# ScalarE copies the last quarter before the new weights in two gate-and-up units of each feed-forward block, and the last down unit adds its kept quarters in a step of its own

## The chip, the core and the metric

The kernel runs on one core of a Trainium2 chip. A core has five engines that run side by side and wait for each other through semaphores: TensorE (PE, matrix products into PSUM; PEld is its weight loads), VectorE (DVE), ScalarE (ACT), GpSimd (POOL) and SyncE (SP, which here only issues DMAs). Each engine takes its instructions in the order in which the program holds them. The metric is the device time of one execution in microseconds. Three runs of the kernel before took 1720.83, 1725.48 and 1731.36 us; their median is 1725.48 us.

## The reference, cut to what matters

Two layers, each with a feed-forward block (FFN), a mixer (convolution and differential attention) and a second FFN; so there are four FFNs. `x` is 512 x 1024, the hidden width `D_FF` is 2816.

```python
def swiglu(h, w_gate, w_up, w_down):
    return (jax.nn.silu(h @ w_gate) * (h @ w_up)) @ w_down
...
    for l in range(DEPTH):
        x = x + 0.5 * swiglu(rms_norm(x, ffn1_norm[l]), ffn1_w_gate[l], ffn1_w_up[l], ffn1_w_down[l])
        h = rms_norm(x, mix_norm[l])
        ...
        x = x + jnp.concatenate([conv_out, diff_out], axis=-1) @ w_out[l]
        x = x + 0.5 * swiglu(rms_norm(x, ffn2_norm[l]), ffn2_w_gate[l], ffn2_w_up[l], ffn2_w_down[l])
    return x
```

## The kernel before

**Precision.** Every float32 operand is split in two rounded parts: ScalarE copies it (`hi`, L375 for the weights of a unit), VectorE takes the rest (`lo`, L379), and TensorE makes three matmuls, hi*hi, hi*lo and lo*hi (`product`, L384 to L394; the matmuls are L392).

**Units.** The 22 tiles of the hidden width are handled in three parts (`PARTS`): 5 plain ones, then 8, then 9. The second and third part are made of *units*. A gate-and-up unit (`GateUp`) makes one hidden tile from 128 columns of the gate and 128 of the up weights; a down unit (`Down`) makes two tiles of the output. A unit is a product of 2 x 2 blocks done with seven block products in place of eight, from sums and differences of the blocks; each product is 4 steps of 3 matmuls on 256 columns. The seven accumulate in the four halves a, d, b, c of two PSUM banks, in this order (`body`, L411 to L446): c, d, then the seventh product of the unit before (`rest`), then a, b, c again ("all") and a again ("g1u2u1"). A half that must be added in twice is copied to SBUF on the way, into four *quarters* of a tile called `keep`: quarter 3 from c (L410), quarters 0 and 1 from a and d (L421), quarter 2 from a after its second product (L442). `rest` of the unit, one unit later, writes into a again, so it must wait until L442 has read a.

**The weights of a unit.** While unit n runs, SyncE loads the weights of unit n+1 (`load`; up L475, gate L476), GpSimd makes four sums of blocks from them (L365 to L368: d, then in place of one up half, then two into the tile `more`), and ScalarE and VectorE split the four operands: A (the up pair, of which the second sum is one half), B (the gate pair), C (`more`, the third and fourth sum) and D (the first sum). The tiles lie in rings: `wraw` has 5 slots and a unit takes three of them (up, gate, more); `whi` and `wlo` have 4 each for A, B and C; D has its own. A slot is given out again in turn, so the up tile of unit n waits for B of unit n-2 to be split, the gate tile of unit n for C of unit n-2, and `more` of unit n for A of unit n-1. The first sum of unit n waits for D of unit n-1 to be split and for the gate tile of unit n.

**What sets the order.** The program is written unit by unit, but a scheduler with a timing model of its own orders the instructions of each engine at build time, except where two are held in the written order (`pinned(..., True)` or `keep_in_program_order`). What it gave for ScalarE and VectorE at the places of the change is shown below. The first matmuls of the products are all held, so the order on TensorE hardly depends on it.

**The places.** A pair of hidden tiles is also summed (`hold`, `combine`), so even and odd units differ a little. The change touches the unit with number n = 3 of the 8 and the one with n = 5 of the 9, in each of four FFNs: eight places. It also touches the last down unit of each FFN, whose `tail` is reversed (a before c): there VectorE in `close` adds quarters 0 and 2 of `keep` to the bank with b and c (L654), adds half of that to one tile of the output `x` (`into`, L644), and `rest` adds to a second tile (L644 again). In the last FFN each tile of `x` is then sent to memory (L1253).

Of the kernel before, what the change touches and what calls it, by code (L numbers as in the profile page):

```python
# [14 lines left out]
AF = mybir.ActivationFunctionType  # L15
ALU = mybir.AluOpType
# [55 lines left out]
def trunk(ctx: ExitStack, tc: tile.TileContext, xt, par, lamv, relb, onehot,  # L72
          gu1, dn1, wag, wqkv, wout, gu2, dn2, out):
    nc = tc.nc
    V, S, G, T = nc.vector, nc.scalar, nc.gpsimd, nc.tensor
# [268 lines left out]
    def pinned(ins, pin=PIN):  # L344
        if pin:
            tc.keep_in_program_order(ins)
        return ins
# [4 lines left out]
    def by_two(t):  # L352
        return t.rearrange("p (n c) -> p n c", n=2)

    class Unit:
# [49 lines left out]
        def body(self, nxt, prev, prev2):  # L405
            if nxt:
                nxt.load()
            self.begin()
            self.go(self.c, "u2u1", "t1", first=True)
            pinned(S.activation(self.keep[:, 3], self.c, AF.Copy))  # L410
            if nxt:  # L411
                nxt.hi("A", isinstance(prev, Down))
                nxt.lo("A")
            self.go(self.d, "u2", "t4", first=True)
            self.early()
            if nxt:
                nxt.hi("B")
            if prev:
                prev.rest()
            self.go(self.a, "g1", "b11")  # L420
            pinned(S.activation(self.keep[:, :2], by_two(self.banks[0]), AF.Copy))  # L421
            if prev:
                prev.finish(0)
            if nxt:
                nxt.lo("B")
            if prev:
                prev.finish(1)
            if nxt:
                nxt.hi("D")
                nxt.lo("D")  # L430
            if prev:
                prev.finish(2)
            self.go(self.b, "g2", "b21")
            self.middle()
            if nxt:
                nxt.hi("C")
            if prev2 and not prev2.soon:
                prev2.combine()
            for ps, *product in self.tail():
                self.go(ps, *product)  # L440
                if ps is self.a:
                    pinned(S.activation(self.keep[:, 2], self.a, AF.Copy), isinstance(self, Down))  # L442
            self.close()
            if nxt:
                nxt.lo("C")
# [18 lines left out]
    class GateUp(Unit):  # L464
# [27 lines left out]
        def close(self):  # L492
            g, two = self.keep[:, 0::2], by_two(self.banks[1])
            pinned(V.tensor_tensor(two, two, g, op=ALU.add))
            pinned(S.activation(g, two, AF.Silu))
# [45 lines left out]
    class Down(Unit):  # L541
# [106 lines left out]
        def close(self):  # L648
            A, B = 2 * self.q, 2 * self.q + 1
            two, keep = by_two(self.banks[1]), self.keep  # L650
            late = self.left and not self.q
            if late:
                self.plain(self.banks[1], 0)
            pinned(V.tensor_tensor(two, two, keep[:, 0::2], op=ALU.add))  # L654
            self.into(A, two, 0.5)
            self.after(A)
            if late:
                self.spare()
            if self.left:
                pinned(V.tensor_tensor(by_two(self.ps), by_two(self.ps), keep[:, 1::2], op=ALU.subtract))  # L660
                self.into(B, by_two(self.ps), 0.5)
# [580 lines left out]
    for l in range(DEPTH):  # L1242
        nxt = {}
# [89 lines left out]
```

## Time and profile before

| what | value |
|---|---|
| the profiled execution, whole | 1723.03 us |
| its span (first to last instruction) | 1721.2 us |
| median of three runs (lowest, highest) | 1725.48 us (1720.83, 1731.36) |
| granted TensorE clock | 1.000 |
| split of unit weights on VectorE, L379, 1024 columns: mean of one | 1454 ns |
| the same on ScalarE, L375, 1024 columns: mean of one | 1062 ns |
| GpSimd's four sums, L365, L366, L367, L368: mean of one | 1221, 1558, 1453, 1523 ns |
| L442, the copy of quarter 2 | 84 times, 352 to 389 ns |

The profiled execution is 2.45 us below the median of the runs. "Idle before" in a row of the profile is the time for which an engine had nothing running just before that instruction, with what ended it. A matmul's row gives its latency; matmuls follow each other faster than they end, so the time of one is read from the distance between starts, or from how many fit in a stretch.

### The profile page before, as it was taken

The page shows a single profiled execution, that of the slowest core. Times are in us where ns is not written, and L with a number is a line of the kernel's source. Part 1 is how long each engine was busy: PE and PEld are TensorE (multiplying, and loading weights), DVE is VectorE, ACT ScalarE, POOL GpSimd, SP SyncE. Part 2 cuts the span into 40 slices and gives each one's busy share as a digit, 9 for nine tenths or more (in the row PEclk, how much of TensorE's full clock was granted, in tenths as well). Part 3 has the DMA queues.
Part 4 walks back from the last instruction along what each step waited for, and adds up shares of the span by engine and source line. Part 5 has one row for each costly group of instructions (what it writes and reads, how often), then busy time and mean ns, then how long its engine had stood idle before and what let it go on. Part 6 is the DMA issues. An engine that isn't in the chain of part 4 may idle for free.

```text
span 1721.2 us, 30788 instructions
## 1 busy us (share of the span) xinstructions
PE 1711.0 (99%) x12013; PEld 1580.8 (92%) x12013; DVE 1404.3 (82%) x2049; ACT 1001.0 (58%) x1607; POOL 894.9 (52%) x664
## 2 busy tenths in 40 slices
PE   9999999999999999999999999999999999999998
PEld 7899999988789899999988999999887888999998
DVE  6988878969766978878968788888688578788887
ACT  6457556645854446656634575665558454565663
POOL 3165555468763146555412566555687531565653
PEclk9999999999999999999999999999999999999999
DMA  7233333433122223333332333334230222333332
GB/s 232 90 113 111 107 109 96 148 106 98 38 74 98 74 98 111 99 120 102 119 103 79 110 107 116 106 111 160 74 111 29 82 87 85 99 116 106 115 107 87
DMA packets 82930, 177.90 MB, mean 103 GB/s; under 512 B 8951, under 2 KB 30726, under 8 KB 82784
## 3 DMA queue, kind: packets, MB, share of 16 engines
q1 hardware_dynamic: 81184, 174.10, 30.6%
q8 instruction: 94, 1.54, 0.4%
q0 software_dynamic: 1312, 1.67, 0.3%
q14 instruction: 52, 0.43, 0.1%
q10 hardware_dynamic: 288, 0.16, 0.0%
HBM read 173.79 MB, written 3.42 MB: 103 GB/s over the span
## 4 chain that ended last, share of the span: by engine, by line
PE 93%; DVE 4%; ACT 1%; issue 1%; DMA 1%; POOL 0%; DVEq 0%; SPq 0%; ACTq 0%
PE ps_pair L392 51%; PE ps_pair L144 6%; PE ps_pair L148 6%; PE ps_pair L147 6%; PE ps_d L144 2%; PE ps_d L147 2%; PE ps_d L148 2%; PE ps_sc L1104 2%; PE ps_out L144 2%; PE ps_out L147 2%; PE ps_out L148 2%; PE ps_pair L980 2%; PE ps_pair L981 2%; PE ps_pair L979 2%; DVE wlo L379 2%; PE ps_o L1134 1%
## 5 line engine op out<-in xcount | busy, mean ns | idle before, releaser
L379 DVE TENSOR_TENSOR wlo<-wraw,whi 128x1024 fp32r<-128x1024 f32 (+1 forms) x400 | 505.0, 1273 | 114.8 <-ACT whi L375 109.0
L375 ACT ACTIVATE whi<-wraw 128x1024 fp32r<-128x1024 f32 (+1 forms) x400 | 375.3, 953 | 215.1 <-PE ps_pair L392 83.2
L365 POOL TENSOR_TENSOR wraw<-wraw 128x512 f32<-128x512 f32 x100 | 122.1, 1221 | 566.1 <-DVE wlo L379 290.0
L392 PE MATMUL ps_pair<-acts,whi 128*128 128x256 f32 x2240 | 393.5, 278 | 0.0
L392 PEld LDWEIGHTS ps_pair<-acts,whi 128*128 128x128 f32 x2240 | 339.8, 188 | 0.4
L392 PE MATMUL ps_pair<-acts,wlo 128*128 128x256 f32 x1120 | 310.8, 278 | 0.0
L392 PE MATMUL ps_pair<-th,whi 128*128 128x256 f32 x816 | 227.1, 278 | 0.4 <-ACT keep L442 0.4
L392 PE MATMUL ps_pair<-tl,whi 128*128 128x256 f32 x816 | 226.5, 278 | 0.0
L392 PE MATMUL ps_pair<-th,wlo 128*128 128x256 f32 x816 | 226.5, 278 | 0.0
L107 ACT ACTIVATE whi<-wraw 128x1024 fp32r<-128x1024 f32 (+3 forms) x124 | 123.5, 1002 | 149.7 <-PE ps_pair L147 83.6
L392 PEld LDWEIGHTS ps_pair<-acts,wlo 128*128 128x128 f32 x1120 | 210.5, 188 | 0.0
L147 PE MATMUL ps_pair<-acts,whi 128*128 128x512 f32 x448 | 174.5, 390 | 0.0
L148 PE MATMUL ps_pair<-acts,wlo 128*128 128x512 f32 x448 | 174.2, 391 | 0.0
L144 PE MATMUL ps_pair<-acts,whi 128*128 128x512 f32 x448 | 173.5, 393 | 0.3 <-ACT whi L107 0.3
L366 POOL TENSOR_TENSOR wraw<-wraw 128x512 f32<-128x512 f32 x100 | 155.8, 1558 | 7.6
L368 POOL TENSOR_TENSOR wraw<-wraw 128x512 f32<-128x512 f32 x100 | 152.3, 1523 | 7.8
L392 PEld LDWEIGHTS ps_pair<-th,whi 128*128 128x128 f32 x816 | 153.2, 188 | 1.2 <-ACT keep L442 0.8
L392 PEld LDWEIGHTS ps_pair<-tl,whi 128*128 128x128 f32 x816 | 154.0, 189 | 0.0
L392 PEld LDWEIGHTS ps_pair<-th,wlo 128*128 128x128 f32 x816 | 153.4, 188 | 0.0
L367 POOL TENSOR_TENSOR wraw<-wraw 128x512 f32<-128x512 f32 x100 | 145.3, 1453 | 7.8
L392 PE MATMUL ps_pair<-hs,whi 128*128 128x256 f32 x704 | 125.3, 278 | 0.0
L1072 DVE SCALAR_TENSOR_TENSOR ps_y<-u,par,ps_y 128x512 f32<-128x512 f32 x156 | 117.6, 754 | 3.8
(220 smaller groups left out, 4080.8 us busy)
## 6 DMA issues: line engine op xcount, KB each, us to landing
wraw<-in_gu SPq DMA_DIRECT2D x172, 512.0 KB, 3.9
wraw<-in_wqkv SPq DMA_DIRECT2D x24, 512.0 KB, 3.8
wraw<-in_wag SPq DMA_DIRECT2D x16, 512.0 KB, 3.8
wraw<-in_wout SPq DMA_DIRECT2D x16, 512.0 KB, 3.6
wraw<-in_dn SPq DMA_DIRECT2D x60, 128.0 KB, 2.9
wraw<-in_dn SPq DMA_DIRECT2D x20, 384.0 KB, 3.2
wraw<-in_dn SPq DMA_DIRECT2D x28, 256.0 KB, 2.9
wraw<-in_dn SPq DMA_DIRECT2D x20, 320.0 KB, 3.0
```

Source lines behind the costliest of these rows:

```text
L107: S.activation(hi, raw, AF.Copy)
L144: first = T.matmul(ps, wh, xh, start=start, stop=False)
L147: T.matmul(ps, wh, xl, start=False, stop=False)
L148: T.matmul(ps, wl, xh, start=False, stop=stop)
L365: G.tensor_tensor(d, g1, u1, op=ALU.add)
L366: G.tensor_tensor(u1, u2, u1, op=ALU.add)
L367: G.tensor_tensor(m0, g1, u1, op=ALU.add)
L368: G.tensor_tensor(m1, g2, m0, op=ALU.add)
L375: pinned(S.activation(hi, raw, AF.Copy), pin)
L379: pinned(V.tensor_tensor(out=lo, in0=raw, in1=f32(hi), op=ALU.subtract), pin)
L392: mm = T.matmul(ps, l, r, start=first and i == n == 0, stop=False, skip_group_check=True)
L1072: V.scalar_tensor_tensor(ys[c] if t == PAD and not n else y, us[c][:, t : t + SEQ], pars[l][:, wc + t : wc + t + 1], y, op0=ALU.mult, op1= ...
```

## The change

Two edits. First, in the unit with n = 3 of the second part and n = 5 of the third, where a gate-and-up unit follows, the copy of C of the next unit is no longer written before the last two products but after them, and L442 and this copy are held in the written order: first quarter 2, then C. Second, in the last down unit of each FFN the addition of quarters 0 and 2 into the PSUM bank is replaced by adding half of them to `x` directly from `keep`, and the bank is added to `x` as before.

```diff
             self.go(self.b, "g2", "b21")
             self.middle()
-            if nxt:
+            swap = isinstance(self, GateUp) and isinstance(nxt, GateUp) and self.n == (3, 5)[self.gated.ahead]
+            if nxt and not swap:
                 nxt.hi("C")
             if prev2 and not prev2.soon:
                 prev2.combine()
             for ps, *product in self.tail():
                 self.go(ps, *product)
                 if ps is self.a:
-                    pinned(S.activation(self.keep[:, 2], self.a, AF.Copy), isinstance(self, Down))
+                    pinned(S.activation(self.keep[:, 2], self.a, AF.Copy), swap or isinstance(self, Down))
+            if swap:
+                nxt.hi("C", True)
             self.close()
             if nxt:
                 nxt.lo("C")
...
-            pinned(V.tensor_tensor(two, two, keep[:, 0::2], op=ALU.add))
+            if self.last:
+                self.into(A, keep[:, 0::2], 0.5)
+            else:
+                pinned(V.tensor_tensor(two, two, keep[:, 0::2], op=ALU.add))
             self.into(A, two, 0.5)
```

**ScalarE at the first place (first FFN, unit n = 3 of the second part).** The unit's keep is `keep_1226`, its banks `ps_pair_1224` (a, d) and `ps_pair_1225` (b, c); `ps_pair_1101` is the unit before (n = 2). `wraw_1219` is C of the next unit (n = 4), `wraw_1348` and `wraw_1349` are A and B of the one after (n = 5). Before:

```order
L421 ACTIVATE keep_1226<-ps_pair_1224 128x512
L375 ACTIVATE whi_1309<-wraw_1219 128x1024
L739 ACTIVATE hold_1287<-ps_pair_1101 128x512
L375 ACTIVATE whi_1374<-wraw_1348 128x1024
L442 ACTIVATE keep_1226<-ps_pair_1224 128x256
L753 ACTIVATE low_183<-ps_pair_1101 128x512
L410 ACTIVATE keep_1360<-ps_pair_1359 128x256
L375 ACTIVATE whi_1390<-wraw_1349 128x1024
L495 ACTIVATE keep_1226<-ps_pair_1225 128x2x256
```

After (lines below the change have moved: L442 is L443, L739 is L745, L753 is L759, L495 is L498):

```order
L421 ACTIVATE keep_1226<-ps_pair_1224 128x512
L745 ACTIVATE hold_1287<-ps_pair_1101 128x512
L759 ACTIVATE low_183<-ps_pair_1101 128x512
L443 ACTIVATE keep_1226<-ps_pair_1224 128x256
L375 ACTIVATE whi_1342<-wraw_1219 128x1024
L375 ACTIVATE whi_1374<-wraw_1348 128x1024
L410 ACTIVATE keep_1360<-ps_pair_1359 128x256
L498 ACTIVATE keep_1226<-ps_pair_1225 128x2x256
L375 ACTIVATE whi_1390<-wraw_1349 128x1024
```

The copies of C (n = 4) and of A (n = 5) have both moved behind the copy of quarter 2; the copy of the hidden tile's parts (L753) has moved ahead of it. The same is so at all eight places.

**VectorE at the same place.** The rows of the unit before, of this one and of the weights. Before:

```order
L502 SCALAR_TENSOR_TENSOR ps_pair_1101<-ps_pair_1101,keep_1103 128x512
L379 TENSOR_TENSOR wlo_1310<-wraw_1219,whi_1309 128x1024
L744 TENSOR_TENSOR ps_pair_1101<-hold_1287,ps_pair_1101 128x256
L379 TENSOR_TENSOR wlo_1375<-wraw_1348,whi_1374 128x1024
L494 TENSOR_TENSOR ps_pair_1225<-ps_pair_1225,keep_1226 128x512
L758 TENSOR_TENSOR low_183<-ps_pair_1101,low_183 128x512
L379 TENSOR_TENSOR wlo_1391<-wraw_1349,whi_1390 128x1024
L500 TENSOR_TENSOR ps_pair_1224<-ps_pair_1224,keep_1226 128x256
L379 TENSOR_TENSOR wlo2_1425<-wraw2_1352,whi2_1424 128x512
L501 TENSOR_TENSOR ps_pair_1224<-ps_pair_1224,keep_1226 128x256
```

After (L744 is L750, L758 is L764, L494 is L497, L500 to L502 are L503 to L505):

```order
L505 SCALAR_TENSOR_TENSOR ps_pair_1101<-ps_pair_1101,keep_1103 128x512
L750 TENSOR_TENSOR ps_pair_1101<-hold_1287,ps_pair_1101 128x256
L764 TENSOR_TENSOR low_183<-ps_pair_1101,low_183 128x512
L497 TENSOR_TENSOR ps_pair_1225<-ps_pair_1225,keep_1226 128x512
L379 TENSOR_TENSOR wlo_1343<-wraw_1219,whi_1342 128x1024
L379 TENSOR_TENSOR wlo_1375<-wraw_1348,whi_1374 128x1024
L503 TENSOR_TENSOR ps_pair_1224<-ps_pair_1224,keep_1226 128x256
L379 TENSOR_TENSOR wlo_1391<-wraw_1349,whi_1390 128x1024
L504 TENSOR_TENSOR ps_pair_1224<-ps_pair_1224,keep_1226 128x256
L379 TENSOR_TENSOR wlo2_1425<-wraw2_1352,whi2_1424 128x512
```

The lo part of C (`wraw_1219`) stood directly behind the last step of the unit before; now it stands three places later, behind the sum that closes unit 3 (L497), which itself waits for quarter 2.

**VectorE at the end of the program (the last down unit, n = q = 3).** `ps_pair_19473` is the bank with b and c, `ps_pair_19472` the one with a. Before:

```order
L660 TENSOR_TENSOR ps_d_19500<-ps_d_19500,keep_19474 128x512
L644 SCALAR_TENSOR_TENSOR x_78<-ps_d_19500,x_78 128x512
L654 TENSOR_TENSOR ps_pair_19473<-ps_pair_19473,keep_19474 128x512
L644 SCALAR_TENSOR_TENSOR x_78<-ps_pair_19473,x_78 128x512
L644 SCALAR_TENSOR_TENSOR x_78<-ps_pair_19472,x_78 128x512
```

After (L660 is L666, L644 is L647):

```order
L666 TENSOR_TENSOR ps_d_19500<-ps_d_19500,keep_19474 128x512
L647 SCALAR_TENSOR_TENSOR x_78<-ps_d_19500,x_78 128x512
L647 SCALAR_TENSOR_TENSOR x_78<-keep_19474,x_78 128x512
L647 SCALAR_TENSOR_TENSOR x_78<-ps_pair_19473,x_78 128x512
L647 SCALAR_TENSOR_TENSOR x_78<-ps_pair_19472,x_78 128x512
```

One instruction is replaced by another in the same place; it no longer reads the bank with b and c. On GpSimd and SyncE nothing moves. On TensorE three matmuls of one step change places with a fourth, once in the program.

## The prediction

> **What bounds the kernel now.** I read the page first, then the waits of TensorE, then its matmul rate by stretches, then the timeline of four engines around one of the eight places. The page's first part:
>
> ```profile
> span 1721.2 us, 30788 instructions
> ...
> PE 1711.0 (99%) x12013; PEld 1580.8 (92%) x12013; DVE 1404.3 (82%) x2049; ACT 1001.0 (58%) x1607; POOL 894.9 (52%) x664
> ```
>
> TensorE is the bound, from end to end; an edit on ScalarE and VectorE can only win what TensorE waits for. Of the seven rows of its waits, this is the one that the change touches:
>
> ```profile
> PE ps_pair L392 <- ACT keep L442: 0.4, 2, 0.2
> ```
>
> Two times, 0.4 us. That undercounts, since a matmul's modelled end covers short gaps. Starts of neighbouring matmuls show more. First at n = 3 in the first FFN of layer 1 and of layer 0, then at n = 5 of both FFNs of layer 1:
>
> ```profile
> 990.09 0.28 PE L392 MATMUL ps_pair<-th,wlo 128*128 128x256 f32 x1
> 990.29 0.38 PE L392 MATMUL ps_pair<-th,whi 128*128 128x256 f32 x1
> ...
> 990.63 0.28 PE L392 MATMUL ps_pair<-th,wlo 128*128 128x256 f32 x1
> ```
>
> ```profile
> 130.55 0.39 PE L392 MATMUL ps_pair<-th,whi 128*128 128x256 f32 x1
> ```
>
> ```profile
> 1123.74 0.28 PE L392 MATMUL ps_pair<-th,wlo 128*128 128x256 f32 x1
> 1124.18 0.38 PE L392 MATMUL ps_pair<-th,whi 128*128 128x256 f32 x1 [0.16 <-ACT keep L442]
> 1124.40 0.28 PE L392 MATMUL ps_pair<-tl,whi 128*128 128x256 f32 x1
> ```
>
> ```profile
> 1645.43 0.39 PE L392 MATMUL ps_pair<-th,whi 128*128 128x256 f32 x1 [0.23 <-ACT keep L442]
> ```
>
> The late matmul is the first of `rest`. What is its cost? That needs the undisturbed rate, from matmuls per stretch:
>
> ```profile
> 95.00:130.00 35.00, 35.00 (x311) 1.00 0.35 112
> 131.00:305.00 174.00, 174.00 (x1480) 1.00 0.32 104
> ...
> 711.00:831.00 120.00, 120.00 (x1022) 1.00 0.33 108
> ...
> 991.00:1123.00 132.00, 132.00 (x1166) 1.00 0.33 109
> ...
> 1512.00:1644.00 132.00, 132.00 (x1165) 1.00 0.33 109
> ```
>
> 132 / 1166 is 113.2 ns a matmul. At 990 three steps took 0.54 us where 0.34 would do: 0.20 lost. At 1123 two took 0.66 for 0.23: 0.43 lost, and by the larger idle time 0.50 at 1645. The other three n = 3 places look like the one at 990, so I take 4 x 0.20 + 0.43 + 0.50 = 1.7 us lost to L442 in the execution.
>
> The same table holds a second thing: 174 / 1480 is 117.6 ns and 120 / 1022 is 117.4, at the same granted clock (1.00, fourth figure). So there is a slow stretch in each FFN of layer 0, together 1480 x 4.4 ns + 1022 x 4.2 ns = 6.5 + 4.3 = 10.8 us, six times the waits. The first begins between 130 and 131, at the late matmul of 130.55; the second begins near 710, where TensorE's waits name nothing. After the n = 3 waits of layer 1, at 990 and just before 1512, the rate stayed at 113.2. So a wait may start a slow stretch (one of the three shown), and a stretch can start without one.
>
> **The first edit.** Why is L442 late? ScalarE and GpSimd around the place at 990:
>
> ```profile
> 984.91 1.06 ACT L375 ACTIVATE whi<-wraw 128x1024 fp32r<-128x1024 f32 x1 [0.59 <-PE ps_pair L392]
> 986.78 0.60 ACT L739 ACTIVATE hold<-ps_pair 128x512 f32<-128x512 f32 x1 [0.81 <-DVE ps_pair L502]
> 988.90 1.06 ACT L375 ACTIVATE whi<-wraw 128x1024 fp32r<-128x1024 f32 x1 [1.52 <-POOL wraw L366]
> 989.87 0.37 ACT L442 ACTIVATE keep<-ps_pair 128x256 f32<-128x256 f32 x1
> ...
> 997.95 1.06 ACT L375 ACTIVATE whi<-wraw 128x1024 fp32r<-128x1024 f32 x1 [1.76 <-POOL wraw L366]
> 998.92 0.36 ACT L442 ACTIVATE keep<-ps_pair 128x256 f32<-128x256 f32 x1
> ```
>
> ```profile
> 985.75 1.09 POOL L365 TENSOR_TENSOR wraw<-wraw 128x512 f32<-128x512 f32 x1 [5.09 <-DVE wlo L379]
> 986.92 1.95 POOL L366 TENSOR_TENSOR wraw<-wraw 128x512 f32<-128x512 f32 x1
> ...
> 994.56 1.10 POOL L365 TENSOR_TENSOR wraw<-wraw 128x512 f32<-128x512 f32 x1 [2.39 <-DVE wlo L379]
> 995.74 2.18 POOL L366 TENSOR_TENSOR wraw<-wraw 128x512 f32<-128x512 f32 x1
> ```
>
> L442 stands behind the copy of A (988.90), which waits for GpSimd's second sum. In the new order only the hold (986.78 to 987.38), a step of VectorE (0.42) and the copy L753 (0.59) stand ahead of L442, so it runs at about 988.4 and ends near 988.75, 1.5 us before TensorE needs it (990.09 + 0.11 = 990.20). The 1.7 us go.
>
> What is late next? The lo part of C. VectorE:
>
> ```profile
> 986.65 1.27 DVE L379 TENSOR_TENSOR wlo<-wraw,whi 128x1024 fp32r<-128x1024 f32 x1
> 987.84 0.42 DVE L744 TENSOR_TENSOR ps_pair<-hold,ps_pair 128x256 f32<-128x256 f32 x1
> 990.00 1.22 DVE L379 TENSOR_TENSOR wlo<-wraw,whi 128x1024 fp32r<-128x1024 f32 x1 [1.74 <-ACT whi L375]
> 991.14 0.69 DVE L494 TENSOR_TENSOR ps_pair<-ps_pair,keep 128x512 f32<-128x512 f32 x1
> ...
> 993.80 0.68 DVE L379 TENSOR_TENSOR wlo<-wraw,whi 128x512 fp32r<-128x512 f32 x1
> ...
> 994.86 0.70 DVE L502 SCALAR_TENSOR_TENSOR ps_pair<-ps_pair,keep 128x512 f32<-128x512 f32 x1
> 995.73 1.23 DVE L379 TENSOR_TENSOR wlo<-wraw,whi 128x1024 fp32r<-128x1024 f32 x1 [0.17 <-ACT whi L375]
> ```
>
> It ended at 987.92 and would now start after the closing sum, at about 989.7. Here a sum of GpSimd and a lo part exclude each other: the sum at 986.92 met the lo part of 986.65 and took 1.95 us for 1.09, ending 0.95 after it; the one at 995.74 took 2.18, ending 0.96 after it. Without a lo part beside them, GpSimd's four sums run 1.09 each from 985.75 with 0.08 between; the fourth spans 989.26 to 990.35, and the lo part of C ends near 991.4, 3.5 us later than before. C itself is needed only at the fifth product from 987.4 (five times 1.36 us), about 994.2: covered. But the gate tile of the unit after next (n = 6) waits for its slot:
>
> ```profile
> 987.95 0.33 SPq L476 DMA_DIRECT2D wraw<-in_gu  x1
> ```
>
> ```profile
> DMA to landing us min/median/max: 3.5/3.7/8.8
> ```
>
> So that load (L476) starts at 991.5, not 987.95, and lands near 995.2. GpSimd's first sum for n = 6 began at 994.56, on the lo part of D; now the landing comes last: 995.2 to 996.3. The next lo part of C (995.55) finds GpSimd busy, ends at 997.3; the second sum, blocked by it, ends 0.95 later, near 998.3 (before: 997.92). A of n = 6 then starts near 998.3, L442 of n = 4 spans 999.3 to 999.65. TensorE needs it 84 matmuls after 990.20, at 999.71, less 0.05 us for the release: no margin. At n = 5 the same chain met TensorE 0.23 us earlier (0.43 lost against 0.20), so 0.2 to 0.3 comes back one unit later. I take 0.05 at four places and 0.25 at the two of layer 1 and at half of the two in layer 0 (in a slow stretch nothing waits): 4 x 0.05 + 3 x 0.25 = 0.95. Bounds: nothing comes back (0), or the landing is late enough (4.1 us and more; the row reaches 8.8) that the lo part goes first. Then the sums end at 996.75 + 1.05 = 997.8 and 998.9, L442 ends at 1000.25, and 0.6 us is lost at n = 3 and 0.8 at n = 5, eight places: 5.6.
>
> **The Trainium skill against this edit.** The skill's page "SBUF — State Buffer", section "Who interferes with whom", has the pair of ports that VectorE shares with GpSimd as an exclusive lock: whoever starts first holds it for the whole instruction, the other blocks. The trace agrees (1.95 and 2.18 us above), and by that rule the moved lo part must pay for GpSimd's fourth sum. Without the rule the lo part would run on from 989.7 to 990.9, the load and all behind it would come 0.5 us sooner, nothing would come back and the sum below would be -1.7 us; with it, -0.75.
>
> **The second edit.** VectorE, ScalarE, TensorE and SyncE at the end of the program:
>
> ```profile
> 1714.38 0.38 ACT L442 ACTIVATE keep<-ps_pair 128x256 f32<-128x256 f32 x1 [2.82 <-PE ps_pair L392]
> ...
> 1715.42 0.28 PE L392 MATMUL ps_pair<-hh,wlo 128*128 128x256 f32 x1
> ...
> 1715.81 0.70 DVE L654 TENSOR_TENSOR ps_pair<-ps_pair,keep 128x512 f32<-128x512 f32 x1 [2.80 <-PE ps_pair L392]
> ...
> 1716.54 1.29 DVE L644 SCALAR_TENSOR_TENSOR x<-ps_pair,x 128x512 f32<-128x512 f32 x2
> ...
> 1716.78 0.28 PE L392 MATMUL ps_pair<-acts,wlo 128*128 128x256 f32 x1
> ```
>
> The new step can run at 1714.8, so the addition of the bank moves from 1716.54 to 1715.81. But the last step waits for TensorE: 0.39 us lie between the start of c's last matmul (1715.42) and VectorE's start (1715.81), so 1716.78 + 0.39 = 1717.17 is its earliest time, and it starts at 1716.54 + 1.29 - 0.69 = 1717.14 already. Gain 0. One output tile leaves 0.7 us earlier; it is not the last one. In the other three FFNs the new step stands where L654 stood, both about 0.7 us. If a sum of GpSimd blocks it (1.1 us), the matmuls of the next stage cover it: its start appears in none of TensorE's waits. 0, at worst 3 x 1.1 = 3.3. The exchange of three matmuls on TensorE costs nothing, the same work issues.
>
> **The sum.** -1.7 + 0.95 + 0 = -0.75 us. On the profiled execution 1723.03 - 0.75 = 1722.3; it stands 2.45 us under the median of the runs, so on the median 1725.48 - 0.75 = 1724.7 us.
>
> **The rivals.** (1) *The wait was the trigger of slow stretches.* Without it the FFN at 130 stays fast: -6.5 us more, 1718.2; if both FFNs of layer 0 do, 1713.9. For it: the change of rate at 130.55. Against: the one at 710 has no such wait, and two of the three waits shown started none. (2) *The late gate load decides (slower).* Place: the unit after each of the eight; it decides once landing takes over 4.1 us or VectorE frees C later than 991.4: 5.6 - 1.7 = 3.9 us more, 1729.4; waits that long may also start a slow stretch of 6.5 us, 1735.9. Against: the median landing of 3.7. (3) *Nothing changes that can be told*, the runs themselves lie 10.5 us apart: 1725.5.
>
> The skill's page "TensorE: Matmul & The Clock Gate", section "Back-to-back issue gap", gives one isolated gap for 256 columns, 109 ns by its formula (an estimate), and no second rate; by it rival (1) could not be and the sum is -0.75. The trace does not agree: it has 113.2 and 117.6.
>
> **How the numbers follow.** The sum as forecast 0.5, its own range 1719 to 1731 (the runs' spread about the median). Rival (1) 0.2, rival (2) 0.17, rival (3) 0.13. A change under 0.5% (8.6 us) can hardly be told from none here, as the runs spread by 0.6%. Faster, under 1716.9: half of (1) and a little of the first, 0.13. Slower, over 1734.1: half of (2) and a little of the first, 0.12. The range reaches to both halves: 1714 to 1734.
>
> **What would show it.** Right: the eight copies of quarter 2 end over 1 us before `rest`, no late matmul there; L476 of the unit after next issues 3.5 us later and its L365 is released by the DMA; a late matmul, at most 0.3 us, one unit on. Wrong: late matmuls of 0.5 us and more there, or slow stretches that go or come with the waits.

## The result, and the profile after

The changed kernel took 1731.95 us (median of 22 runs, 1724.83 to 1735.9), the kernel before 1728.01 us (22 runs, 1720.82 to 1732.6). The ratio is 1.0028, 95% interval 1.0017 to 1.004: slower, by 4.8 us (2.9 to 6.9), where -0.75 us had been forecast. (The ratio and its interval are the ones on record; they are not the quotient of the two medians, which is 1.0023.) The profiled execution of the changed kernel took 1731.63 us, 8.6 more than the one of before. About half of these 8.6 us lies in the choice of executions: the one of before, 1723.03 us, is 5.0 us under the median of its 22 runs, the changed one 0.3 under its own. Its page begins

```profile
span 1729.9 us, 30780 instructions
...
PE 1720.1 (99%) x12013; PEld 1590.2 (92%) x12013; DVE 1409.9 (82%) x2049; ACT 999.8 (58%) x1607; POOL 872.3 (50%) x664
```

TensorE has the same 12013 matmuls and is busy 9.1 us longer. So the time did not come as waits that the profile names. All of TensorE's waits that the profile names (engine, line, waited for; us in total, times, longest):

```profile
PE ps_o L1140 <- DVE acts L1171: 1.6, 2, 0.8
PE ps_sc L1110 <- DVE e L1124: 1.4, 4, 0.5
PE ps_idle L175 <- DVE relb L885: 1.0, 1, 1.0
PE ps_pair L144 <- ACT whi L107: 0.6, 1, 0.6
PE ps_sc L1110 <- DVE mn L1114: 0.5, 2, 0.3
```

The row on the copy of quarter 2 (L442, now L443) has gone, as it should. The copy itself, and the matmul that used to be late, at the n = 3 place of the third FFN (ScalarE, then TensorE):

```profile
986.47 0.38 ACT L443 ACTIVATE keep<-ps_pair 128x256 f32<-128x256 f32 x1
```

```profile
988.22 0.28 PE L392 MATMUL ps_pair<-th,wlo 128*128 128x256 f32 x1
988.33 0.28 PE L392 MATMUL ps_pair<-th,whi 128*128 128x256 f32 x1
```

The copy ends at 986.85, 1.48 us early, and the matmul of 988.33 comes in step. One unit later it is late. In the fourth FFN it is late one unit later too (0.17 us lost, the pace after it unchanged), and again two units later. The places at which the pace then changes:

```profile
997.74 0.28 PE L392 MATMUL ps_pair<-th,wlo 128*128 128x256 f32 x1
997.94 0.38 PE L392 MATMUL ps_pair<-th,whi 128*128 128x256 f32 x1
998.16 0.28 PE L392 MATMUL ps_pair<-tl,whi 128*128 128x256 f32 x1
...
1534.07 0.28 PE L392 MATMUL ps_pair<-th,wlo 128*128 128x256 f32 x1
1534.18 0.35 PE L392 MATMUL ps_pair<-th,whi 128*128 128x256 f32 x1
1534.37 0.28 PE L392 MATMUL ps_pair<-tl,whi 128*128 128x256 f32 x1
```

At 997.94 two steps took 0.42 us where 0.23 would do, 0.20 lost; at 1534.18 one step took 0.19 for 0.11, 0.07 lost. These are too small for the view of waits. What they did to TensorE stands in the matmuls per stretch (stretch, its length, busy time and count, clock); of before, and of after:

```profile
106.00:176.00 70.00, 70.00 (x604) 1.00 0.35 112
...
1002.00:1036.00 34.00, 34.00 (x303) 1.00 0.34 109
...
1610.00:1670.00 60.00, 59.77 (x527) 1.00 0.35 115
```

```profile
106.00:176.00 70.00, 70.00 (x618) 1.00 0.36 112
...
1002.00:1036.00 34.00, 34.00 (x291) 1.00 0.36 109
...
1610.00:1670.00 60.00, 60.00 (x512) 1.00 0.34 106
```

From 1002 us 34 us held 303 matmuls before and 291 after, at the same clock; from 106 us it is the other way round, 604 and 618. From one matmul's start to the next, in the trace's nanoseconds, TensorE has two paces for 256 columns: 113.3 ns and 117.8 ns, and little between. Before, the units had slow stretches from 130.9 to 307.9 us and from 710 to 834 us; after, from 182 to 306, 708 to 832, **999 to 1166 and 1534 to 1691**. The two new ones begin at the two late matmuls shown. Their excess is (1166 - 999) x 3.8% = 6.4 and (1691 - 1534) x 3.8% = 6.0 us, where 3.8% is 4.5 / 117.8; against them stand 2.0 us from 131 to 182, which run fast now.

Below, *excess* is the sum, over the matmuls of 256 columns whose next one starts within 160 ns, of that distance less 113.3 ns: 13.1 us before, 22.9 after. By this the pace costs 9.9 us more in this pair of executions. Span less excess is 1708.1 and 1707.0. That 1.1 us can't be told from nothing: the kernel of experiment 2, which has none of the late matmuls at the eight places either, stands at 1708.2, and the granted clock of the profiled executions lies between 0.998 and 1.000, where a thousandth of 1720 us is 1.7 us.

### The profile page after: what moved, and what is told of

Read it like the earlier page. It is cut to its first block, busy times and chain, and to the rows that moved or that the text cites. A ratio compares the mean times of both kernels' runs of the same rounds, so it can differ in the third digit from the quotient of the medians.

```text
span 1729.9 us, 30780 instructions
## 1 busy us (share of the span) xinstructions
PE 1720.1 (99%) x12013; PEld 1590.2 (92%) x12013; DVE 1409.9 (82%) x2049; ACT 999.8 (58%) x1607; POOL 872.3 (50%) x664
## 3 DMA queue, kind: packets, MB, share of 16 engines
q1 hardware_dynamic: 81184, 174.10, 31.6%
## 4 chain that ended last, share of the span: by engine, by line
PE 95%; DVE 2%; ACT 1%; DMA 1%; issue 0%; POOL 0%; SPq 0%; ACTq 0%; DVEq 0%; POOLq 0%
PE ps_pair L392 54%; PE ps_pair L144 6%; PE ps_pair L148 6%; PE ps_pair L147 6%; PE ps_d L147 2%; PE ps_d L144 2%; PE ps_d L148 2%; PE ps_sc L1110 2%; PE ps_out L144 2%; PE ps_out L148 2%; PE ps_out L147 2%; PE ps_pair L986 2%; PE ps_pair L985 2%; PE ps_pair L987 2%; PE ps_o L1140 1%; PE ps_v L1017 1%
## 5 line engine op out<-in xcount | busy, mean ns | idle before, releaser
L365 POOL TENSOR_TENSOR wraw<-wraw 128x512 f32<-128x512 f32 x100 | 118.0, 1180 | 598.1 <-DVE wlo L379 288.9
L107 ACT ACTIVATE whi<-wraw 128x1024 fp32r<-128x1024 f32 (+3 forms) x124 | 123.3, 1002 | 149.4 <-PE ps_pair L147 83.7
L366 POOL TENSOR_TENSOR wraw<-wraw 128x512 f32<-128x512 f32 x100 | 147.6, 1476 | 7.6
L367 POOL TENSOR_TENSOR wraw<-wraw 128x512 f32<-128x512 f32 x100 | 146.4, 1464 | 7.8
L368 POOL TENSOR_TENSOR wraw<-wraw 128x512 f32<-128x512 f32 x100 | 140.5, 1405 | 7.8
```

The source lines that it names most:

```text
L107: S.activation(hi, raw, AF.Copy)
L365: G.tensor_tensor(d, g1, u1, op=ALU.add)
L366: G.tensor_tensor(u1, u2, u1, op=ALU.add)
L367: G.tensor_tensor(m0, g1, u1, op=ALU.add)
L368: G.tensor_tensor(m1, g2, m0, op=ALU.add)
```

## The experiments

The theory: a wait that TensorE meets by a hair throws it into the slow pace, and the edit, which removes six waits (two of the eight places, in the slow stretches of layer 0, had none), leaves smaller ones in the next two units. Rivals: the second edit costs the time; or the pace follows from what ScalarE, VectorE and GpSimd do beside TensorE, not from waits. All ratios are to the kernel before, with 95% intervals.

| kernel | median us | ratio | profiled span | excess | span less excess |
|---|---|---|---|---|---|
| before | 1728.01 | 1 | 1721.2 | 13.1 | 1708.1 |
| changed | 1731.95 | 1.0028 (1.0017 to 1.004) | 1729.9 | 22.9 | 1707.0 |
| first edit alone | 1730.15 | 1.0034 (1.0019 to 1.0049) | 1734.3 | 25.5 | 1708.8 |
| copy first | 1719.82 | 0.9972 (0.9962 to 0.9981) | 1718.5 | 10.3 | 1708.2 |
| copy first, second edit | 1719.88 | 0.9972 (0.9959 to 0.9986) | 1717.7 | 11.0 | 1706.7 |
| changed, copy first in two more units | 1725.46 | 1.0001 (0.9987 to 1.0015) | 1724.2 | 10.5 | 1713.7 |
| changed, 16 matmuls of 512 | 1734.84 | 1.0057 (1.0034 to 1.008) | 1730.5 | 15.9 | 1714.6 |
| changed, 16 matmuls of 256 | 1733.79 | 1.0051 (1.0035 to 1.0067) | 1729.0 | 13.2 | 1715.8 |
| copy first, 4 matmuls of 512 in fast stretches | 1741.14 | 1.0092 (1.007 to 1.0114) | 1738.9 | 31.6 | 1707.3 |
| copy first, 2 matmuls of 512 in slow stretches | 1714.02 | 0.9938 (0.9917 to 0.9959) | 1712.2 | 4.6 | 1707.6 |
| copy first, extra copy, no wait | 1719.29 | 0.9954 (0.9936 to 0.9972) | 1716.5 | 10.3 | 1706.2 |
| copy first, extra copy, a hair | 1733.3 | 1.0024 (1.001 to 1.0038) | 1732.5 | 24.2 | 1708.3 |
| copy first, extra copies, 0.5 us of wait | 1726.71 | 0.9998 (0.998 to 1.0016) | 1720.7 | 11.1 | 1709.6 |

The medians of before in the four sets of runs are 1728.01, 1724.59 (runs 1, 2 and 3 below), 1724.7 (4, 5, 6) and 1727.9 us (7).

### 1. The first edit alone

The changed kernel with its second edit undone.

```diff
-            if self.last:
-                self.into(A, keep[:, 0::2], 0.5)
-            else:
-                pinned(V.tensor_tensor(two, two, keep[:, 0::2], op=ALU.add))
+            pinned(V.tensor_tensor(two, two, keep[:, 0::2], op=ALU.add))
```

> The first edit alone (the copies of the gate-up units exchanged; the last unit as before). Theory, the pace: a matmul of 256 columns repeats after 113.3 ns or after 117.8 ns, and the profile after has 22.9 us of such excess over 113.3 ns against 13.0 us before; the late gate loads make small waits one and two units later, and these start slow stretches at about 997 and 1534 us. Then this kernel is as the changed one, 1.0028 of before (1.0015 to 1.0045), with slow stretches that begin in the two units after the exchanged copy. Rival, the second edit costs the time: 1.000 (0.9985 to 1.001).

1.0034 (1.0019 to 1.0049): a loss as large as that of both edits is here, and the second edit is cleared. Matmuls per stretch of this kernel:

```profile
151.00:300.00 149.00, 149.00 (x1267) 1.00 0.33 103
1012.00:1160.00 148.00, 148.00 (x1259) 1.00 0.34 104
1540.00:1690.00 150.00, 150.00 (x1276) 1.00 0.33 103
```

All of these are at 117.6 ns. The slow stretches begin at about 150, 667, 1010 and 1538 us, each at a late matmul in the two units behind an exchanged copy, but not all at the same places as in the profile of the two edits together: which of the small waits starts one differs between these executions.

### 2. The copy first, the C weights where they were

The kernel before; at the eight places L442 is held ahead of the copy of A of the unit after next, and nothing of C moves.

```diff
-                nxt.hi("A", isinstance(prev, Down))
+                nxt.hi("A", isinstance(prev, Down) or getattr(prev, "swap", False))
...
+            self.swap = isinstance(self, GateUp) and isinstance(nxt, GateUp) and self.n == (3, 5)[self.gated.ahead]
...
-                    pinned(S.activation(self.keep[:, 2], self.a, AF.Copy), isinstance(self, Down))
+                    pinned(S.activation(self.keep[:, 2], self.a, AF.Copy), self.swap or isinstance(self, Down))
```

> The kernel before, with one thing changed at the same 8 places: the copy of the last quarter is put ahead of the copy of the A weights of the unit after next, as the changed kernel has it, but copy and subtraction of the C weights stay where they were, so no load starts late. Theory, the pace: the waits on the last quarter go and none come back one or two units later, so nothing starts a slow stretch there: 1.7 us of waits are saved, and up to 6.5 us more where a stretch like that of 131 to 308 us does not start: 0.997 of before (0.994 to 0.9995). Rival, the order of the engines beside TensorE sets its pace: no forecast, within 0.9985 and 1.003. Rival, early copies of the last quarter are themselves bad (ScalarE later with A): over 1.000.

0.9972 (0.9962 to 0.9981), on the forecast of 0.997. Twelve runs lie between 1719.06 and 1721.4 us, 2.3 us apart, where those of before lie 7.4 apart. SyncE and ScalarE at the place that answers to 997.94 of the changed kernel:

```profile
986.17 0.33 SPq L477 DMA_DIRECT2D wraw<-in_gu  x1
```

```profile
995.97 1.06 ACT L375 ACTIVATE whi<-wraw 128x1024 fp32r<-128x1024 f32 x1 [1.67 <-POOL wraw L366]
996.94 0.36 ACT L443 ACTIVATE keep<-ps_pair 128x256 f32<-128x256 f32 x1
```

TensorE needs this copy at 997.95, and it ends at 997.30, 0.65 us early. In the changed kernel the same load, the same sum and the same copy read

```profile
989.56 0.34 SPq L479 DMA_DIRECT2D wraw<-in_gu  x1
```

```profile
993.39 1.09 POOL L365 TENSOR_TENSOR wraw<-wraw 128x512 f32<-128x512 f32 x1 [4.94 <-DMA wraw<-in_gu]
994.56 1.97 POOL L366 TENSOR_TENSOR wraw<-wraw 128x512 f32<-128x512 f32 x1
```

```profile
996.56 1.06 ACT L375 ACTIVATE whi<-wraw 128x1024 fp32r<-128x1024 f32 x1 [2.26 <-POOL wraw L366]
997.53 0.36 ACT L443 ACTIVATE keep<-ps_pair 128x256 f32<-128x256 f32 x1
```

with the copy needed at about the same time, 997.85. The gate load issues 3.4 us later, the first sum is released by the DMA, and the copy of quarter 2 comes 0.59 us later: 0.65 us to spare have become nothing. So the first half of the exchange is good, and its second half, C behind it, is what lost the time. A sixth slot in the ring of raw weights for the late load, with the rest of the changed kernel left alone, was not run.

### 3. Sixteen matmuls of another width

The changed kernel with added work that nothing reads: one matmul in the gate-and-up units n = 6 of the second and n = 7 of the third part, and in each second down unit (q = 1), four per FFN.

```diff
             if prev:
                 prev.rest()
+            if self.n == ((6, 7)[self.gated.ahead] if isinstance(self, GateUp) else -1) or isinstance(self, Down) and self.q == 1:
+                self.wide()
...
+        def wide(self):
+            x512 = self.halves.hi[:, 0, :] if isinstance(self, GateUp) else self.h.hh[0][0]
+            ps = bank("tp", "ps_wide")[:, :512]
+            tc.keep_in_program_order(T.matmul(ps, self.weights("u2", 0)[0], x512[:, :512], start=True, stop=True))
...
+            self.n = None
```

> The changed kernel with 16 matmuls of 512 columns added (work that nothing reads): one in each FFN's unit three places after the exchanged copy, one in each second down unit; 16 x 0.227 us = 3.6 us of TensorE time. Theory, the pace: slow stretches end at matmuls of 512 columns, as they do at about 306, 832, 1166 and 1691 us in the profile after, so the stretches that begin at 182, 708, 999 and 1534 us end within three units of their start, and the excess falls from 22.9 to some 7 us: 0.9928 of before for a profiled execution like that of the changed kernel (0.990 to 0.997). Rival, the pace comes from what runs beside TensorE: the stretches stay and the 3.6 us come on top, 1.005 of before (1.003 to 1.007).

> As the run with 16 added matmuls of 512 columns, at the same places, but with 256 columns each (work that nothing reads); 16 x 0.113 us = 1.8 us of TensorE time. If it is the width that ends a slow stretch, these end none: 1.004 of before (1.002 to 1.006). If any added matmul outside the products' rhythm, or the scheduler's small moves on the other engines that come with it, ends them, this kernel is as fast as the one with 512 columns, 0.990 to 0.997.

Neither is faster than the changed kernel: 1.0057 and 1.0051 against 1.0028, with intervals that overlap its own. So the forecast of 0.9928 failed. Two reasons. First, the additions made waits of their own (for the split weights of the unpaired ninth tile, `nine`; at quarter 2; and for the bank that the added matmuls write), 2.5 us with 512 columns and 3.8 us with 256 in the view of waits, beside their 3.6 and 1.8 us of work. Second, the theory was wrong on the width. Around two of the added matmuls (L402) of 512 columns:

```profile
716.79 0.28 PE L392 MATMUL ps_pair<-hs,wlo 128*128 128x256 f32 x1
716.91 0.39 PE L402 MATMUL ps_wide<-low,whi 128*128 128x512 f32 x1
717.14 0.39 PE L392 MATMUL ps_pair<-low,whi 128*128 128x256 f32 x2
717.37 0.28 PE L392 MATMUL ps_pair<-low,wlo 128*128 128x256 f32 x1
...
1535.10 0.28 PE L392 MATMUL ps_pair<-th,wlo 128*128 128x256 f32 x1
1535.22 0.39 PE L402 MATMUL ps_wide<-acts,whi 128*128 128x512 f32 x1
1535.44 0.40 PE L392 MATMUL ps_pair<-acts,whi 128*128 128x256 f32 x2
1535.68 0.28 PE L392 MATMUL ps_pair<-acts,wlo 128*128 128x256 f32 x1
```

At 716.91 the pace goes from 118 to 113 ns, at 1535.22 from 113 to 118 (0.24 us for two matmuls). Such a matmul ends a slow stretch (7 of the 9 met in one), but it also starts one (3 of the 4 met in a fast one that had no wait of their own). With 256 columns none of the 13 without a wait changed the pace. So the width acts, but in both directions.

### 4. One matmul of 512 columns, in a fast and in a slow stretch

To settle that, on the steady kernel of experiment 2, with the same matmul (work that nothing reads) in one kernel in fast stretches, at unit n = 1 of the second part, four in all (first diff); in the other in slow ones, at n = 2 of the third part in layer 0 alone, two in all (the condition of the second diff, with the same matmul under it):

```diff
+            if isinstance(self, GateUp) and self.n == 1 and not self.gated.ahead:
+                ps = bank("tp", "ps_one")
+                tc.keep_in_program_order(
+                    T.matmul(ps, self.weights("u2", 0)[0], self.halves.hi[:, 0, :], start=True, stop=True))
```

```diff
+            if isinstance(self, GateUp) and self.n == 2 and self.gated.ahead and self.halves.l == 0:
```

> The run that put the copy first at 8 places, with one matmul of 512 columns added in the second unit of each FFN (about 103, 630, 961 and 1481 us; work that nothing reads), all in a stretch at 113.3 ns; 4 x 0.227 us = 0.9 us of work. If TensorE has two lasting paces between which such a matmul switches (behind the 16 added ones it went from 117.8 to 113.3 ns in most places, and from 113.3 to 117.8 ns at 1136 and 1535 us), the slow pace holds from there until the first down unit at least (80 us in each FFN): 320 us at 4% is 12.2 us, and 21 us if it holds to 1165 and 1690 us in the last two: 1.005 to 1.010 of before. If the pace does not hang on it: 0.9977.

> The run that put the copy first at 8 places, with one matmul of 512 columns (work that nothing reads) in each of the first layer's two FFNs, in the third gate-up unit of the second part (about 237 and 763 us), in the middle of the slow stretches of 182 to 305 and 709 to 832 us; 2 x 0.227 = 0.45 us of work. If it switches the pace, the stretch from there to the next down unit (about 40 us each) runs at 113.3 ns: 2 x 40 x 3.8% = 3.0 us less, 0.9957 of before; to the end of the stretches (68 us each) 5.2 us less, 0.9945. If the pace does not hang on it: 0.9975.

Four matmuls of 0.23 us in fast stretches cost 21.3 us (1741.14 against 1719.82); two in slow stretches, in layer 0 alone, gain 5.8 us (1714.02), which makes this the fastest kernel of all: 0.9938 of before (0.9917 to 0.9959). Matmuls per stretch of the run without them (experiment 2), of the one with four, of the one with two:

```profile
106.00:176.00 70.00, 70.00 (x620) 1.00 0.36 113
232.00:300.00 68.00, 68.00 (x580) 1.00 0.35 106
1002.00:1036.00 34.00, 34.00 (x302) 1.00 0.36 109
```

```profile
106.00:176.00 70.00, 70.00 (x597) 1.00 0.35 110
...
1002.00:1036.00 34.00, 34.00 (x291) 1.00 0.36 109
```

```profile
232.00:300.00 68.00, 68.00 (x602) 1.00 0.36 109
```

All four switched to slow, and it held to the end of the FFN (103 to 310, 632 to 838, 967 to 1172, 1495 to 1704 us); both of the others switched to fast, and it held to the end too. That ScalarE, VectorE and GpSimd set the pace can't be upheld: they do the same work in the same order but for at most 35 of their 4320 instructions, and TensorE's pace follows one matmul.

### 5. The changed kernel with the copy first in the next two units

The late loads stay; L443 is put ahead of the copy of A in the units n = 4, 5 of the second part and 6, 7 of the third too, so that it no longer waits behind them.

```diff
+            self.near = n in ((4, 5), (6, 7))[gated.ahead]
...
-                nxt.hi("A", isinstance(prev, Down))
+                nxt.hi("A", isinstance(prev, Down) or isinstance(prev, GateUp) and prev.near)
...
-                    pinned(S.activation(self.keep[:, 2], self.a, AF.Copy), swap or isinstance(self, Down))
+                    pinned(S.activation(self.keep[:, 2], self.a, AF.Copy), swap or isinstance(self, Down) or self.near)
```

> The changed kernel, with the copy of the last quarter put ahead of the A weights' copy also in the two units behind each exchanged one (8 x 2 units); the late subtraction of C and the late gate loads stay. If the small waits on that copy in these units are what costs the time, they go and so do the slow stretches that began at them: 0.9975 of before (0.996 to 0.999), like the run that put the copy first at 8 places. If the late loads, or the order on ScalarE and VectorE that the change brings, set TensorE's pace in another way: 1.003 (1.0015 to 1.0045), as the changed kernel.

1.0001 (0.9987 to 1.0015): between the two forecasts. The pace is what the theory says, an excess of 10.5 us as in experiment 2 (10.3), with no slow stretch from 999 or 1534:

```profile
1002.00:1036.00 34.00, 34.00 (x302) 1.00 0.36 109
```

But the late loads now push other work late, and TensorE waits for that: for the quarter 2 of the last paired unit (L537) and for the `nine` tile.

```profile
PE ps_pair L392 <- ACT keep L537: 2.1, 4, 0.7
PE ps_pair L392 <- DVE nine L724: 1.8, 4, 0.5
```

3.9 us against 0.6 in experiment 2. The waits on quarter 2 made the slow stretches of the changed kernel, but the late loads are not free without them.

### 6. The second edit, on the steady kernel

```diff
+            if self.last:
+                self.into(A, keep[:, 0::2], 0.5)
+            else:
+                pinned(V.tensor_tensor(two, two, keep[:, 0::2], op=ALU.add))
-            pinned(V.tensor_tensor(two, two, keep[:, 0::2], op=ALU.add))
             self.into(A, two, 0.5)
```

> The run that put the copy first at 8 places, with the change's second edit on top (the last unit adds its kept quarters early). The second edit costs nothing by the prediction: 0.9972 of before again (0.996 to 0.998). If VectorE's last step were on the end's path: up to 0.2 points below (0.9952).

0.9972 (0.9959 to 0.9986), medians 1719.88 against 1719.82: it costs and gains nothing.

### 7. A wait by a hair, made on purpose

On the kernel of experiment 2 the copy of quarter 2 of unit n = 4 ends 0.65 us early in all four FFNs. ScalarE gets one more copy ahead of it, which nothing reads, of a length chosen to leave 0.38 us, about nothing, or -0.5 us.

```diff
+                    extra = isinstance(self, GateUp) and self.n == 4 and not self.gated.ahead
+                    if extra:
+                        wide = bank("tp", "ps_extra")
+                        pinned(S.activation(wide[:, :480], self.banks[0][:, :480], AF.Copy, accum_out=wide[:, 511:]), True)
-                    pinned(S.activation(self.keep[:, 2], self.a, AF.Copy), self.swap or isinstance(self, Down))
+                    pinned(S.activation(self.keep[:, 2], self.a, AF.Copy), self.swap or extra or isinstance(self, Down))
```

That is the middle one; the small one copies 256 columns without the accumulated output, the long one copies 256 columns twice.

> The run that put the copy first at 8 places, with a copy by ScalarE that nothing reads (256 columns from PSUM, some 0.27 us of its time behind another) put directly ahead of the copy of the last quarter in the fifth gate-up unit of each FFN (at about 139, 665, 997 and 1518 us). There the copy ends 0.65 us before TensorE comes to the matmul that needs it, in all four places; 0.38 us of that is left. All theories: no wait, nothing slower: 0.9972 of before (0.996 to 0.9985), slow stretches as in the run without it.

> As the run with the small extra copy, at the same 4 places, but with one of 480 columns and an accumulated output, some 0.47 + 0.2 us: the copy of the last quarter ends about as TensorE comes to need it, and the wait is between nothing and 0.1 us. If a wait by a hair starts a slow stretch by itself: slow from about 140, 666, 998 and 1519 us to the first down unit at least (43 us each, 1.7 us), in the last two FFNs perhaps to 1165 and 1690 us (6.5 us each): 1.001 to 1.007 of before. If such waits start none, and the stretches of the changed kernel come from something else that it moves: 0.9975 (0.996 to 0.9985).

> As the run with the small extra copy, at the same 4 places, but with two copies of 256 columns, between which ScalarE makes another that it has to make (0.63 us): the copy of the last quarter ends some 0.4 us after TensorE comes to need it; 4 x 0.4 = 1.6 us of waits. If only a wait by a hair starts a slow stretch, as the waits of 0.23 us and more at 666, 1124 and 1645 us in the profiles of the changed kernel and of before let one think: 0.9982 of before (0.997 to 0.9995). If any wait starts one: 1.002 to 1.008.

The small one left everything as it was (1719.29 us against 1719.82). The middle one cost 14 us more than the small one: 1733.3 us, 1.0024 of before (1.001 to 1.0038). Its place in the fourth FFN on TensorE, and one of its stretches:

```profile
1526.77 0.28 PE L392 MATMUL ps_pair<-th,wlo 128*128 128x256 f32 x1
1526.88 0.33 PE L392 MATMUL ps_pair<-th,whi 128*128 128x256 f32 x1
1527.05 0.28 PE L392 MATMUL ps_pair<-tl,whi 128*128 128x256 f32 x1
```

```profile
1610.00:1670.00 60.00, 60.00 (x512) 1.00 0.36 112
```

The step at 1526.88 is 0.16 us for 0.11: 0.05 us lost. From it TensorE runs at 118 ns until 1695. Three of the four places started a slow stretch (140.7, 1000.5 and 1526.9; not 668.7). Four waits of 0.05 to 0.07 us, 0.2 us together, cost 14.

The long one has four waits of 0.5 us:

```profile
139.83 0.28 PE L392 MATMUL ps_pair<-th,wlo 128*128 128x256 f32 x1
140.46 0.38 PE L392 MATMUL ps_pair<-th,whi 128*128 128x256 f32 x1 [0.36 <-ACT keep L446]
140.68 0.28 PE L392 MATMUL ps_pair<-tl,whi 128*128 128x256 f32 x1
```

0.52 and 0.11 lost in two steps, 2.5 us over the four; the profiled execution took 1722.52 us, 2.7 more than the median of experiment 2, and shows no slow stretch begun there. But its twelve runs spread from 1721.62 to 1734.57, with a median of 1726.71, ratio 0.9998 (0.998 to 1.0016). A second profiled execution was meant to catch a longer one:

> The kernel with the two extra copies once more, for another profiled execution. Its profiled execution took 1722.5 us and none of the four waits of about 0.5 us started a slow stretch, but its other executions lie between 1721.6 and 1734.6 us, median 1726.7. If longer waits start the slow pace in some executions, one of more than 1725 us shows a slow stretch that begins at one or two of the four places (about 140, 667, 999 and 1520 us); one of 1721 to 1723 us shows none, as before. If the spread has another source, an execution of more than 1725 us shows longer waits elsewhere and no new slow stretch.

It took 1722.81 us, and again none of the four waits started a slow stretch. So eight long waits of eight seen started none, while the longer executions, which no profile caught, must lose time somewhere: whether a long wait sometimes starts one stays open.

All the profiled executions here (14, of 13 kernels) can be asked the same. They hold 59 places in the products of the gate-and-up units at which a matmul started over 130 ns after the one before (one such step or two in a row), all of them in the fast pace. By the time lost there, over 113.3 ns a step:

| lost at the place | places | slow pace from there on |
|---|---|---|
| 0.05 to 0.10 us | 20 | 11 |
| 0.10 to 0.25 us | 17 | 4 |
| 0.27 to 1.11 us | 22 | 0 |

Only three of the 15 starts are behind an added copy of ScalarE, so the added copy itself is not what starts it. Why some of the short waits do and others of the same length do not is not shown.

## Why the prediction was wrong, by its own steps

| step | predicted | measured |
|---|---|---|
| the late matmuls at the eight places (six before) go | 1.7 us won | all gone |
| L442 ends before it is needed | 1.5 us | 1.48 us (988.33 - 986.85) |
| the gate load issues later, against TensorE's place | 3.5 us | 3.5 us |
| it then releases the first sum | DMA in place of VectorE | DMA |
| L442 of the next unit, end against need | 0.06 us early, no margin | 0.04 us late (997.89 against 997.85) |
| lost there, one unit later | 4 x 0.05 us | 0.09, 0.35, 0.20, 0.17 = 0.81 us |
| lost at other places | 3 x 0.25 us, at n = 5 | 3 x 0.07 = 0.2 us, two units after n = 3 |
| sum of what comes back | 0.95 us | 1.0 us |
| second edit | 0 | 0 |
| pace of the matmuls | no term | +9.9 us in the profiled execution |

For the third row: the load issued 2.25 us before `rest` of the exchanged unit (987.95 against 990.20), and now 1.23 us after it (989.56 against 988.33). The chain of the first edit held link by link. That the waits which came back cost in sum what was forecast is luck. One unit after n = 3 they cost four times the forecast (0.81 against 0.20). One unit after n = 5 nothing was lost, because all four of these places now lie in slow stretches, where TensorE asks later. Where that stretch ran fast, in three cases of experiment 3, the same place lost 0.44, 0.55 and 1.11 us against the 0.25 forecast (those kernels have added matmuls in other units too); the largest, in the kernel with 16 matmuls of 256 columns:

```profile
1661.80 0.39 PE L392 MATMUL ps_pair<-th,whi 128*128 128x256 f32 x1 [0.84 <-ACT keep L450]
```

**The step that failed is the pricing of "0.95 us comes back".** It priced a wait by its length. The prediction had seen that "a wait may start a slow stretch", but put this in the rivals alone: in rival (1) for the wait of 0.19 us at 130.55, which goes, and for waits that come back in rival (2) alone, which let waits of 0.6 to 0.8 us start one, while the forecast's own 0.05 us started none. For the waits that come back the runs show the reverse. Waits of 0.05 to 0.2 us are those that start a slow stretch (997.94 and 1534.18 after; 15 of the 37 places of up to 0.25 us, and none of the 22 longer ones, in the table of experiment 7), and the two such waits of the changed profile cost 6.4 and 6.0 us, thirty to ninety times their length. In the sum, the forecast had no term for this at all. The forecast put L442 of the next unit at "no margin", the one place where that is worst, and took the smallest price for it.

**Rival (1)**, that the wait at 130.55 was the trigger of the stretch from 131 to 305, was right for a third of it. Without that wait 131 to 182 runs fast (x620 in place of x604 from 106 to 176, experiment 2), but from 182 on it is slow again in both kernels and in every profile here: another start lies in the first down unit, with no late matmul. So 2 us hung on the wait, not 6.5; experiment 2, with its 0.9972, is this rival's outcome. **Rival (2)** was right in sign, by the slow stretch and not by its long waits: its condition, a landing later than 4.1 us, was not met, as GpSimd's first sum began 3.7 to 4.0 us after the load at all eight places. The time lies inside the range given, and +0.28% is within the 0.5% that the prediction held to be hardly told from none; with 22 runs of each it can be told, and the sign was missed.

## What to carry to other kernels

Where TensorE runs from end to end, count matmuls per stretch in every profile, not only waits: two kernels with the same matmuls differed here by 9 us, in a row that says 99% busy both times. An operand that arrives just as TensorE needs it is worse than one that is late by half a microsecond in the runs seen, so an edit that leaves "no margin" somewhere is to be priced by the slow stretch it can start, or be changed so that a margin is left (here: move one copy ahead, and leave the other where it is). If a slow stretch can't be avoided, one matmul of another width in its middle may end it; in a fast stretch the same matmul does the harm.

## What the runs showed of the hardware

- Matmuls of 256 float32 columns in three-matmul steps, each with its own weights, run at one of two paces, 113.3 or 117.8 ns, at a granted clock of 1.00 both times; TensorE stays in one for 100 us and more. In the trace each weight load starts 3 to 4 ns after the matmul before it in both paces; the matmul follows its load by 110 ns in the fast pace and by 114 to 115 in the slow one.
- Waits of 0.05 to 0.2 us started the slow pace at 997.94, at 1534.18 and at three of four made on purpose; others of the same size did not (139.77, 149.40, 675.74 after). In all the profiles, 15 of 37 places that lost up to 0.25 us started it, and none of 22 that lost more.
- One matmul of 512 columns among those of 256 turns the pace over: fast to slow in four of four, slow to fast in two of two, and 10 of 13 in the run with sixteen. One of 256 columns does not (0 of 13).
- The start in the first down unit (about 182 and 708 us) is not explained. There some matmuls on the tile `hs` take 116 to 118 ns; in layer 0 the slow pace stays, in layer 1 it goes back after three or four matmuls, one of them of 122 to 124 ns (experiment 2 and others). No run tested it.
